# Hybrid decoder layer: the mixer's gates, queries and keys in seven-product groups

## The chip, the cores and the metric

The kernel runs on one core of a Trainium2 chip. The metric is the device time of one execution in microseconds (us). A core has five engines with queues of their own: TensorE (PE in the profile, its weight loads PEld), VectorE (DVE), ScalarE (ACT), GpSimd (POOL) and SyncE (SP). Each engine takes its instructions strictly in the order in which they were placed, and waits where an instruction's inputs or its output buffer are not ready. Transfers between DRAM and the on-chip memory are issued by SP and POOL.

## The reference, cut to what matters

One layer over 256 tokens of width 2048: a feed-forward half step (FFN), a mixer with two attention branches, a second FFN, each followed by a layer norm of the residual sum. Everything is float32. The mixer:

```python
def _mixer(h, positions, w_in, ...):
    c_q, c_kv, k_r, dq, dk, dv, gate_mla, gate_diff = _split_columns(h @ w_in)   # 512, 512, 64, 1024, 1024, 1024, 2048, 2048
    q = (_rms_norm(c_q, q_norm_g) @ w_uq).reshape(b, s, MLA_HEADS, MLA_QK_DIM)   # then rope on a part
    c_kv = _rms_norm(c_kv, kv_norm_g)
    k_nope = (c_kv @ w_uk).reshape(...)
    v_mla = (c_kv @ w_uv).reshape(...)
    ...
    o_mla = _mla_attention(q, k, v_mla).reshape(b, s, MLA_V_COLS)
    o_diff = _diff_attention(dq, dk, dv, positions, lam)                         # reshaped by heads
    o_diff = (_rms_norm(o_diff, subln_g) * (1.0 - lambda_init)).reshape(b, s, DIFF_V_COLS)
    y = jax.nn.sigmoid(gate_mla) * (o_mla @ w_br_mla) + jax.nn.sigmoid(gate_diff) * (o_diff @ w_br_diff)
    return y @ w_out
```

## The kernel before, in words

**Products.** A float32 product is made of three passes: activations and weights are each split into a rounded part `hi` and a rest `lo`, and `triple` (lines 201 to 204) multiplies hi by hi, hi by lo and lo by hi into one PSUM bank. The split of a weight tile of 128 x 1024 (`split`, lines 148 to 150) is a copy on ScalarE (L149) and a subtraction on VectorE (L150). Activations (128 tokens of one half b) are the stationary operand, weights the moving one, 512 columns wide.

**Units.** `project` (L206) goes over one chunk of 512 columns in units of two input tiles (G = 2): load of 512 KB by SyncE into one of four `raw` buffers, split into a pair of the ring (`wring`), then 12 matmuls: 2 tiles x 2 token halves x 3 passes. A chunk over the whole width of 2048 (16 tiles, KD) is 8 units, a chunk over 512 (4 tiles) is 2. `unit`, `advance` and `look` (lines 167 to 190) keep two queues: `look(3, 4)` makes the program place loads three units ahead of the split, and splits four units ahead of the matmuls; with `look(0, 0)` they stand directly one behind the other. Engines run ahead of each other in any case as far as the ring (six pairs in the mixer, after `narrow_to(6)`) allows.

**Due times.** `later(n, fn)` puts work off by n units, `tick` runs it. A planner then orders the instructions of each engine by its own estimate of when their inputs are ready, so that a piece that is due later may be placed earlier on an engine.

**Seven products.** `Hybrid` (L290) takes two chunks of 512 columns together. Over the first 8 of 16 input tiles it treats tokens, inputs and columns as 2 x 2 blocks and forms seven block products in place of eight (`Seven`, L249, prepares the sums of activation blocks from the float32 copies `x.raws`; weight blocks are added on VectorE, L333). The other 8 tiles go by plain units. The raw weight blocks 11, 12, 21 and 22 of 128 x 1024 have two buffers each (`sraw`), and partial banks are kept as snapshots (`snap`, L310 and L311, copies on ScalarE). `group` runs 14 half products and 8 plain units. Both FFNs use it for their gate and up weights; `Folded` is a like scheme for the down weights, in which block 21 shares block 12's buffers (additions at L434).

**Memory.** `act_tile` gives one of 40 slots of 128 x 1024 floats, `tmp_tile` one of 6 slots of 128 x 512. PSUM has 5 banks for products and 3 for the rest.

**Turning.** Rows (tokens on partitions) become columns through DRAM: `turn` (L533) transposes 32 x 32 blocks on VectorE (L525), stores them by four POOL transfers (L527, `turn<-blocks`), loads them back (L539, `turned<-turn`), and then copies or splits them (L547, or `put`).

**The mixer** (L839) runs in this order: the compressed rows c_q (chunk `wc0`) and c_kv with k_r (`wc1`, `wc2`), normalized and turned at once into `cn`; diff queries `dqT` (2 chunks); `wuq` (3 chunks of 2 units), `wuk`, `wuv`; then diff keys `dkT`, diff values `dv`; then `gate(0)`, `gate(1)`, and for f = 0 to 3 `branch(f)` followed by `gate(f + 2)`. Each gate is two chunks (`wgm`, `wgd`), kept in an `act_tile` until its branch multiplies it in. The pieces of the attention heads (`mla_head`, `diff_head`) are strewn between the units by `later`. All of it goes by plain `project`.

Of the kernel before, what the change touches and what calls it, by code (L numbers as in the profile page):

```python
# [18 lines left out]
P = 128  # L19
# [40 lines left out]
def layer_kernel(ctx: ExitStack, tc: tile.TileContext, a: dict, out: bass.AP):  # L60
# [102 lines left out]
    def catch_up(n):  # L163
        while len(behind) > n:
            behind.popleft()()
# [124 lines left out]
    class Hybrid:  # L290


        def __init__(self, x, seven, k_tiles):
            self.x, self.seven, self.k_tiles = x, seven, k_tiles
            self.raws = {n: [act_tile([P, 1024], F32, "sraw") for _ in range(2)] for n in ("11", "12", "21", "22")}
            self.snaps = [[act_tile([P, 2, 512], F32, "snap") for _ in range(2)] for _ in range(2)]
            self.turn = 0

        def group(self, w0, w1, done):
            banks = {}  # L300
            snap = [t[:, i, :] for t in self.snaps[self.turn % 2] for i in range(2)]
            self.turn += 1
            n1, n2, n3, q5 = snap
            R = self.raws
# [534 lines left out]
    def mixer(x):  # L839
# [2 lines left out]
        gain = act_tile([P, 1024], F32, "gain")  # L842
        nc.gpsimd.dma_start(gain, a["c_gain"].partition_broadcast(P))
        cn = Acts(8, "cn")
        krT = act_tile([P, 2, T], F32, "krT")

        def c_norm(b, i):
            c = c_row[b][:, i * RANK:(i + 1) * RANK]
            junk = tmp_tile([P, RANK], "junk")
            ss = sm(1, "ss")  # L850
            S.activation(junk, c, AF.Square, accum_out=ss)
            ms = sm(1, "ms")
            V.tensor_scalar(out=ms, in0=ss, scalar1=1.0 / RANK, scalar2=None, op0=ALU.mult)
            r = rstd(ms, RMS_EPS, 1)
            V.scalar_tensor_tensor(out=c, in0=c, scalar=r, in1=gain[:, i * RANK:(i + 1) * RANK],
                                   op0=ALU.mult, op1=ALU.mult)
            later(2, lambda: turn_to_quad(c, b, cn, i, 4, 8))

        def cq_done(b, bank):
            S.copy(c_row[b][:, 0:RANK], bank)  # L860
# [27 lines left out]
            project(w, xx, kt, 512, done, k0)  # L888
            return dst

        def rows_proj(ws, xx, kt, name, k0=0):
            dst = [act_tile([P, 1024], F32, name) for _ in range(2)]

            def done(c, b, bank):
                S.copy(dst[b][:, c * 512:(c + 1) * 512], bank)
            for c in range(2):
                project(ws[c], xx, kt, 512, lambda b, bank, c=c: done(c, b, bank), k0)
            return dst
# [12 lines left out]
        v = rows_proj(a["wuv"], cn, 4, "v", 4)  # L911

        om = Acts(MH, "om")
        od = Acts(MH, "od")
# [96 lines left out]
        def gate(f):  # L1011
            for i, w in enumerate((a["wgm"], a["wgd"])):
                gt = act_tile([P, 2, 512], F32, "gate")

                def done(b, bank, gt=gt):
                    S.copy(gt[:, b, :], bank)
                project(w[f], x, KD, 512, done)
                gates[f, i] = gt

        yq = Acts(KD, "y")  # L1020

        def branch(f):
            g0, g1 = gates[f, 0], gates[f, 1]

            def done0(b, bank):
                V.tensor_tensor(out=g0[:, b, :], in0=bank, in1=g0[:, b, :], op=ALU.mult)

            def done1(b, bank):
                V.tensor_tensor(out=g1[:, b, :], in0=bank, in1=g1[:, b, :], op=ALU.mult)
                V.tensor_tensor(out=g0[:, b, :], in0=g0[:, b, :], in1=g1[:, b, :], op=ALU.add)  # L1030
                if f < 2:
                    later(1, lambda: turn_to_quad(g0[:, b, :], b, yq, f, 4, 6))
                else:
                    later(2, lambda: rows_to_quad(g0[:, b, :], b, yq, f))
            catch_up(0)
            for t in (g0, g1):
                S.activation(t, t, AF.Sigmoid)
            project(a["wbm"][f], om, MH, 512, done0)
            project(a["wbd"][f], od, MH, 512, done1)
# [138 lines left out]
```

## Time and profile before

| what | value |
|---|---|
| median of three runs | 2008.99 us (2007.35 to 2014.54) |
| profiled execution | 2005.43 us, its span 2003.7 us |
| TensorE busy | 1987.9 us, 99% |
| VectorE busy | 1629.5 us, 81% |
| ScalarE busy | 1191.2 us, 59% |
| GpSimd busy | 238.7 us, 12% |
| DRAM traffic | 455.25 MB, mean 227 GB/s |

The first FFN takes about the first 690 us, the mixer lasts until about 1190, the output projection until about 1300, and the second FFN fills the rest. Rows by stretch give the busy time of each engine with its number of instructions in brackets, then the granted TensorE clock, the share of the transfer engines, and GB/s. Rows in order of time give start and duration in us; in square brackets stands how long the engine was idle before the row and what it waited for. Matmuls are pipelined, so their durations overlap; the steps from start to start tell what one costs.

### The profile page before, as it was taken

What the parts mean: (1) busy time and instruction counts of PE and PEld (TensorE: products, weight loads), DVE (VectorE), ACT (ScalarE), POOL (GpSimd) and SP (SyncE); (2) the same over time, 40 slices, a digit from 0 to 9 for tenths busy, and PEclk for the clock granted to TensorE, in tenths of its full rate; (3) what the DMA queues carried; (4) which work ended last, traced back from release to release, by engine and by line L of the source; (5) the groups of instructions that cost most, each with busy time, mean ns of one, the idle gap of its engine ahead of it and who ended that gap; (6) DMA issues with size and microseconds to landing.
All of it is one profiled execution on the core that took longest, in us unless ns stands there. A gap on an engine that the chain in (4) does not pass through costs nothing.

```text
span 2003.7 us, 25261 instructions
## 1 busy us (share of the span) xinstructions
PE 1987.9 (99%) x8928; PEld 1646.3 (82%) x8928; DVE 1629.5 (81%) x1922; ACT 1191.2 (59%) x1503; POOL 238.7 (12%) x443
## 2 busy tenths in 40 slices
PE   9999999999999999999999999999999999999997
PEld 7888888888888898788888888888888888888886
DVE  8999999998897676565665555699999999987875
ACT  6666666666655564555764444466666666665551
POOL 0111001012100013520001100001110110121000
PEclk9999999999999999999999999999999999999999
DMA  8667656668777667864456675666676666588673
GB/s 325 218 225 266 236 193 217 222 200 279 269 270 234 201 216 242 288 226 157 148 179 215 213 276 189 218 223 230 223 268 230 198 215 230 195 290 288 220 241 112
DMA packets 132048, 455.25 MB, mean 227 GB/s; under 512 B 19105, under 2 KB 19153, under 8 KB 131921
## 3 DMA queue, kind: packets, MB, share of 16 engines
q1 hardware_dynamic: 109296, 389.59, 57.0%
q0 software_dynamic: 22624, 64.04, 10.3%
q8 instruction: 70, 1.15, 0.2%
q14 instruction: 58, 0.47, 0.1%
HBM read 428.92 MB, written 24.64 MB: 226 GB/s over the span
## 4 chain that ended last, share of the span: by engine, by line
PE 91%; DMA 4%; DVE 1%; issue 1%; ACT 1%; POOL 1%; SPq 0%; DVEq 0%; ACTq 0%; POOLq 0%
PE mm L204 29%; PE mm L202 29%; PE mm L203 29%; DMA turn<-blocks 2%; DMA turned<-turn 1%; PE tr L202 1%; PE tr L203 1%; PE tr L204 1%; POOL turn L527 1%; DVE wring L150 1%; ACT wring L149 1%; DMA raw<-in_wdq_dram 1%; PE tr L490 0%; DMA raw<-in_wdk_dram 0%; DMA raw<-in_gu_dram 0%
## 5 line engine op out<-in xcount | busy, mean ns | idle before, releaser
L150 DVE TENSOR_TENSOR wring<-raw,wring 128x1024 fp32r<-128x1024 f32 (+2 forms) x551 | 660.8, 1205 | 263.3 <-ACT wring L149 257.1
L149 ACT CAST wring<-raw 128x1024 fp32r<-128x1024 f32 (+2 forms) x551 | 570.0, 1040 | 417.6 <-PE mm L204 322.3
L202 PE MATMUL mm<-wring,h 128*128 128x512 f32 (+2 forms) x1504 | 584.5, 389 | 0.0
L204 PE MATMUL mm<-wring,h 128*128 128x512 f32 (+2 forms) x1504 | 580.1, 386 | 0.0
L203 PE MATMUL mm<-wring,h 128*128 128x512 f32 (+2 forms) x1504 | 579.2, 385 | 0.0
L149 ACT CAST wring<-sraw 128x1024 fp32r<-128x1024 f32 x336 | 349.8, 1053 | 147.9 <-PE mm L204 93.3
L150 DVE TENSOR_TENSOR wring<-sraw,wring 128x1024 fp32r<-128x1024 f32 x336 | 403.4, 1218 | 9.6 <-ACT wring L149 5.0
L204 PEld LDWEIGHTS mm<-wring,h 128*128 128x128 f32 x1504 | 282.4, 188 | 57.5 <-DVE h L150 1.0
L202 PEld LDWEIGHTS mm<-wring,h 128*128 128x128 f32 x1504 | 282.6, 188 | 56.0 <-ACT h L149 1.0
L203 PEld LDWEIGHTS mm<-wring,h 128*128 128x128 f32 x1504 | 282.6, 188 | 55.6 <-DVE wring L150 0.2
L202 PE MATMUL mm<-wring,xs 128*128 128x512 f32 x608 | 236.5, 389 | 0.0
L203 PE MATMUL mm<-wring,xs 128*128 128x512 f32 x608 | 236.5, 389 | 0.0
L204 PE MATMUL mm<-wring,xs 128*128 128x512 f32 x608 | 236.5, 389 | 0.0
L333 DVE TENSOR_TENSOR sraw<-sraw,sraw 128x1024 f32<-128x1024 f32 x160 | 192.3, 1212 | 0.0
L527 POOL DMA_DIRECT2D hT<-blocks x176 | 95.9, 553 | 759.6 <-DVE blocks L525 705.3
L203 PE MATMUL mm<-wring,x 128*128 128x512 f32 x384 | 149.7, 390 | 0.6 <-DVE wring L150 0.6
L202 PE MATMUL mm<-wring,x 128*128 128x512 f32 x384 | 149.4, 390 | 0.6 <-ACT wring L149 0.6
L204 PE MATMUL mm<-wring,x 128*128 128x512 f32 x384 | 149.3, 389 | 0.0
L203 PEld LDWEIGHTS mm<-wring,xs 128*128 128x128 f32 x608 | 114.1, 188 | 23.7
L202 PEld LDWEIGHTS mm<-wring,xs 128*128 128x128 f32 x608 | 114.1, 188 | 23.7
L204 PEld LDWEIGHTS mm<-wring,xs 128*128 128x128 f32 x608 | 114.1, 188 | 23.7
L527 POOL DMA_DIRECT2D turn<-blocks x104 | 56.9, 554 | 305.6 <-DVE blocks L525 261.3
(252 smaller groups left out, 1850.3 us busy)
## 6 DMA issues: line engine op xcount, KB each, us to landing
raw<-in_gu_dram SPq DMA_DIRECT2D x191, 512.0 KB, 4.3
sraw<-in_gu_dram SPq DMA_DIRECT2D x160, 512.0 KB, 5.3
raw<-in_dn_dram SPq DMA_DIRECT2D x144, 512.0 KB, 4.5
hraw<-hT POOLq DMA_DIRECT2D x80, 256.0 KB, 4.7
sraw<-in_dn_dram SPq DMA_DIRECT2D x32, 512.0 KB, 5.5
raw<-in_wgm_dram SPq DMA_DIRECT2D x32, 512.0 KB, 3.3
raw<-in_wgd_dram SPq DMA_DIRECT2D x32, 512.0 KB, 3.8
raw<-in_w_out_dram SPq DMA_DIRECT2D x32, 512.0 KB, 3.4
```

Source lines behind the costliest of these rows:

```text
L149: S.copy(hi, src)
L150: V.tensor_tensor(out=lo, in0=src, in1=hi.bitcast(F32), op=ALU.subtract)
L202: PE.matmul(o, xh, wh, start=first, stop=False, skip_group_check=again)
L203: PE.matmul(o, xh, wl, start=False, stop=False, skip_group_check=again)
L204: PE.matmul(o, xl, wh, start=False, stop=last, skip_group_check=again)
L333: V.tensor_tensor(out=t, in0=t, in1=R[add[1]][s], op=ALU.add)
L527: nc.gpsimd.dma_start(to.rearrange("(g r) (i f) -> i r g f", g=4, i=4)[i], t[32 * i:32 * (i + 1), :].rearrange("r (g f) -> r g f", g=4))
```

## The change

The mixer opens differently. After the compressed rows, the first halves of the two gates (chunks 0 and 1 of `wgm` and of `wgd`), the diff queries and the diff keys go as four pairs of chunks through `Hybrid`. For this the activations of the first two quarters are kept in float32 (`h1 = Acts(KD, "h1", (0, 1))`), and the sums of `Seven` are made while the compressed rows are projected. `Hybrid` gets a `small` form: block 21 shares block 12's two buffers, there is one set of snapshots, and the last three products come in the order 3, 2, 4. `look(3, 4)` holds for the four groups, `look(0, 0)` after them.

All gates (16 tiles of 128 x 512) go to DRAM and are loaded again before their branch. The compressed rows also wait in DRAM, and are loaded and split during the first half of the diff values, which now stands ahead of `wuq`; the second half follows after `wuv`, then the other halves of the gates by plain `project`. A branch is divided: `branch_mla` copies its product to a tile, `branch_diff` multiplies in both gates and adds. The due times of the heads change.

```diff
-        def __init__(self, x, seven, k_tiles):
+        def __init__(self, x, seven, k_tiles, small=False):
+
             self.x, self.seven, self.k_tiles = x, seven, k_tiles
-            self.raws = {n: [act_tile([P, 1024], F32, "sraw") for _ in range(2)] for n in ("11", "12", "21", "22")}
-            self.snaps = [[act_tile([P, 2, 512], F32, "snap") for _ in range(2)] for _ in range(2)]
+            self.raws = {n: [act_tile([P, 1024], F32, "sraw") for _ in range(2)] for n in ("11", "12", "22")}
+            self.raws["21"] = self.raws["12"] if small else [act_tile([P, 1024], F32, "sraw") for _ in range(2)]
+            self.snaps = [[act_tile([P, 2, 512], F32, "snap") for _ in range(2)] for _ in range(1 if small else 2)]
+            self.last = (3, 2, 4) if small else (2, 4, 3)
...
-            for p, n, j in ((1, 0, 4), (5, 0, 5), (6, 0, 6), (7, 0, 7), (2, 1, 4), (4, 1, 5), (3, 1, 6)):
+            for p, n, j in zip((1, 5, 6, 7) + self.last, (0, 0, 0, 0, 1, 1, 1), (4, 5, 6, 7, 4, 5, 6)):
...
+        turns = {}
+        seven = Seven(x.raws)
+        for i, f in enumerate(seven.steps):
+            later(14 + 2 * i, f)
...
-            later(2, lambda: turn_to_quad(c, b, cn, i, 4, 8))
+            turns[i, b] = dram.tile([P, 512], F32, name=nm("turn"))
+            later(2, lambda: turn_out(c, turns[i, b]))
...
+        gate_rows = dram.tile([4, 2, 2, P, 512], F32, name="gates")
+
+        def keep_gate(i, f, b, bank, snap=None, op=None):
+            t = tmp_tile([P, 512], "gate")
+            if snap is None:
+                S.copy(t, bank)
+            else:
+                V.tensor_tensor(out=t, in0=bank, in1=snap, op=op)
+            nc.gpsimd.dma_start(gate_rows[f, i, b], t)
+
+        look(3, 4)
+        hy = Hybrid(x, seven, KD, True)
+        for i, w in enumerate((a["wgm"], a["wgd"])):
+            hy.group(w[0], w[1], lambda n, b, bank, snap, op, i=i: keep_gate(i, n, b, bank, snap, op))
+
+        def pair_cols(w, name):
+            dst = [act_tile([P, 4, T], F32, name) for _ in range(2)]
+
+            def done(n, b, bank, snap, op):
+                t = tmp_tile([P, 512], name + "r")
+                V.tensor_tensor(out=t, in0=bank, in1=snap, op=op)
+                later(1, lambda: turn_to_cols(t, dst[n], b, 4, 10))
+            hy.group(w[0], w[1], done)
+            return dst
+
+        dqT = pair_cols(a["wdq"], "dqT")
+        dkT = pair_cols(a["wdk"], "dkT")
+        look(0, 0)
...
-        dqT = [cols_proj(a["wdq"][c], x, KD, "dqT") for c in range(2)]
+        def c_back(j):
+            if j == 0:
+                for key, src in turns.items():
+                    back[key] = tmp_tile([P, 512], "turned")
+                    nc.gpsimd.dma_start(back[key], src)
+            if j >= 4:
+                i, b = divmod(j - 4, 2)
+                cn.put(i, b, turned(back[i, b]))
+
+        dv, dv_part = rows_proj("dv")
+        dv_part(a["wdv"], x, KD, 0, 0, c_back)
...
-                later(12 + 3 * h + 2 * i, f)
-        dkT = [cols_proj(a["wdk"][c], x, KD, "dkT") for c in range(2)]
-        dv = rows_proj(a["wdv"], x, KD, "dv")
+                later(10 + 3 * h + 2 * i, f)
...
-                later(4 + 6 * h + 3 * i, f)
+                later(22 + 6 * h + 3 * i, f)
...
+        for f, at in enumerate((44, 48, 56, 60)):
+            later(at, lambda f=f: get_gates(f))
+
+        dv_part(a["wdv"], x, KD, 1)
+        for i, w in enumerate((a["wgm"], a["wgd"])):
+            for f in (2, 3):
+                project(w[f], x, KD, 512, lambda b, bank, i=i, f=f: keep_gate(i, f, b, bank))
...
-        gate(0)
-        gate(1)
-        for f in range(4):
-            branch(f)
-            if f + 2 < 4:
-                gate(f + 2)
+        for f in range(3):
+            branch_mla(f)
+        branch_diff(0)
+        branch_diff(1)
+        branch_mla(3)
+        branch_diff(2)
+        branch_diff(3)
...
-    h1 = Acts(KD, "h1")
+    h1 = Acts(KD, "h1", (0, 1))
```

More of the change, by code (lines that the diff above doesn't have):

```diff
@@ L300, in group @@
             banks = {}
-            snap = [t[:, i, :] for t in self.snaps[self.turn % 2] for i in range(2)]
+            snap = [t[:, i, :] for t in self.snaps[self.turn % len(self.snaps)] for i in range(2)]
             self.turn += 1
@@ new lines, in rows_proj, with part, done @@
+        def rows_proj(name):
+            dst = [act_tile([P, 1024], F32, name) for _ in range(2)]
+            def part(ws, xx, kt, c, k0=0, hook=None):
+                def done(b, bank):
+                    S.copy(dst[b][:, c * 512:(c + 1) * 512], bank)
+                project(ws[c], xx, kt, 512, done, k0, hook)
+            return dst, part
+        back = {}
+        def c_back(j):
[6 more added lines that the diff above has]
+                cn.put(i, b, turned(back[i, b]))
@@ L910, in mixer @@
         kT = [cols_proj(a["wuk"][c], cn, 4, "kT", 4, 8) for c in range(2)]
-        v = rows_proj(a["wuv"], cn, 4, "v", 4)
+        v, v_part = rows_proj("v")
+        for c in range(2):
+            v_part(a["wuv"], cn, 4, c, 4)
         om = Acts(MH, "om")
@@ L1020, in mixer, with get_gates @@
-        yq = Acts(KD, "y")
[L1022 to L1035, printed above, removed]
+        def get_gates(f):
+            gates[f] = [act_tile([P, 2, 512], F32, "gate") for _ in range(2)]
+            for i, t in enumerate(gates[f]):
+                for b in range(2):
+                    nc.gpsimd.dma_start(t[:, b, :], gate_rows[f, i, b])
@@ L1036, in branch, with branch_diff, done @@
+        def branch_diff(f):
+            g0, g1 = gates.pop(f)
+            y = mla_rows.pop(f)
             for t in (g0, g1):
                 S.activation(t, t, AF.Sigmoid)
-            project(a["wbm"][f], om, MH, 512, done0)
-            project(a["wbd"][f], od, MH, 512, done1)
-        gate(0)
-        gate(1)
-        for f in range(4):
-            branch(f)
-            if f + 2 < 4:
-                gate(f + 2)
+            def done(b, bank):
+                V.tensor_tensor(out=y[:, b, :], in0=y[:, b, :], in1=g0[:, b, :], op=ALU.mult)
+                V.tensor_tensor(out=g1[:, b, :], in0=bank, in1=g1[:, b, :], op=ALU.mult)
+                V.tensor_tensor(out=y[:, b, :], in0=y[:, b, :], in1=g1[:, b, :], op=ALU.add)
+                if f < 2:
+                    later(1, lambda: turn_to_quad(y[:, b, :], b, yq, f, 4, 6))
+                else:
+                    later(2, lambda: rows_to_quad(y[:, b, :], b, yq, f))
+            project(a["wbd"][f], od, MH, 512, done)
```

17 lines of the change are left out of this document (4 added, 13 removed).

## The prediction

> **What bounds the kernel now.** I read the profile's page first (busy shares, slices), then the busy time by stretch, then single engines in order of time, and last the waits.
>
> ```profile
> span 2003.7 us, 25261 instructions
> PE 1987.9 (99%) x8928; PEld 1646.3 (82%) x8928; DVE 1629.5 (81%) x1922; ACT 1191.2 (59%) x1503; POOL 238.7 (12%) x443
> PEclk9999999999999999999999999999999999999999
> ```
> ```profile
> core 0: us, PE busy (x) PEld busy (x) DVE busy (x) ACT busy (x) POOL busy (x), PEclk, DMA share, GB/s
> 400.00:450.00 50.00, 50.00 (x222) 41.38 (x222) 48.79 (x54) 32.95 (x39) 6.55 (x12) 1.00 0.61 204
> 710.00:750.00 40.00, 40.00 (x257) 37.47 (x256) 26.76 (x56) 24.15 (x46) 6.60 (x12) 1.00 0.73 240
> 780.00:790.00 10.00, 9.14 (x40) 7.04 (x39) 1.88 (x2) 3.72 (x5) 1.14 (x2) 1.00 0.53 205
> 1100.00:1150.00 50.00, 50.00 (x222) 41.42 (x221) 28.41 (x29) 23.05 (x26) 6.04 (x11) 1.00 0.65 205
> ```
> ```profile
> 700.00:1200.00 500.00, 497.40 (x2336) 414.92 (x2335) 303.48 (x479) 274.65 (x425) 80.13 (x146) 1.00 0.66 216
> ```
>
> TensorE bounds every stage. The stretch at 400 lies in the first FFN's hybrid groups, where VectorE is 98% busy; the one at 1100 lies in the mixer's gates, where VectorE is 57% busy; both pass 222 matmuls in 50 us. So a VectorE at 98% does not yet slow TensorE here. In the mixer (700 to 1200) TensorE is idle for only 2.6 us in all.
>
> What one matmul is worth is not its duration:
>
> ```profile
> 1099.77 0.39 PE L203 MATMUL mm<-wring,h 128*128 128x512 f32 x1
> ...
> 1101.36 0.39 PE L204 MATMUL mm<-wring,h 128*128 128x512 f32 x1
> ```
>
> Seven starts follow each other in 1.59 us between these rows: 0.227 us per matmul, while each lasts 0.39. Pricing by the duration would overstate the gain 1.7 times.
>
> **The change, part by part.**
>
> *Matmuls.* Two chunks of 512 columns over 16 input tiles cost 2 x 16 x 2 halves x 3 products = 192 matmuls. A hybrid group costs 7 x 4 x 3 = 84 for the first eight tiles and 96 for the rest: 180. Four groups save 48; in the instruction order of the two programs 8424 matmuls of 512 columns become 8376 and every other TensorE count stays. 48 x 0.227 = **10.9 us** off the bounding engine.
>
> *VectorE and ScalarE.* A group splits 22 weight tiles where 16 were split, and adds 8 pairs of weight tiles.
>
> ```profile
> L150 DVE TENSOR_TENSOR wring<-sraw,wring 128x1024 fp32r<-128x1024 f32 x336 | 403.4, 1218 | 9.6 <-ACT wring L149 5.0
> L333 DVE TENSOR_TENSOR sraw<-sraw,sraw 128x1024 f32<-128x1024 f32 x160 | 192.3, 1212 | 0.0
> L647 DVE TENSOR_TENSOR gus<-mm,snap 128x512 f32<-128x512 f32 x80 | 54.6, 682 | 0.0
> L525 DVE STREAM_TRANSPOSE blocks<-dqTr 128x512 f32<-128x512 f32 x4 | 2.8, 702 | 0.0
> L149 ACT CAST wring<-sraw 128x1024 fp32r<-128x1024 f32 x336 | 349.8, 1053 | 147.9 <-PE mm L204 93.3
> L310 ACT COPY snap<-mm 128x512 f32<-128x512 f32 x40 | 23.3, 583 | 9.9 <-PE mm L204 9.9
> ```
> ```profile
> 426.09 3.49 DVE L150 TENSOR_TENSOR wring<-sraw,wring 128x1024 fp32r<-128x1024 f32 x3
> ```
>
> Neighbours overlap: three splits take 3.49 us, so each after the first adds (3.49 - 1.22) / 2 = 1.135, 0.08 less than its duration; I take 0.08 off the others too. A gate group then needs 30 x 1.135 + 4 x 0.60 = 36.5 us of VectorE against 180 x 0.227 = 40.9 of TensorE (89%). A group of queries or keys adds 4 transposes of 0.62: 38.9 us (95%). An FFN group by the same sum has 36.5 + 4 x 0.34 + 2 x 0.61 = 39.1 (96%), and there the row above shows no loss. ScalarE needs 22 x 0.97 + 4 x 0.5 = 23 us, little over half. The five preparation steps of the products (four subtractions, three splits, a negation: about 6.4 us of VectorE by the same prices) fall into 710 to 750, where VectorE has 13.2 us free in the row above. Inside the first group also fall the norm and rotation of the second compressed half, about 6.5 us. So over four groups VectorE has 163.6 - 36.5 x 2 - 38.9 x 2 - 6.5 = 6.3 us to spare, besides its lead: four units prepared ahead, at 40.9 / 22 units = 7.4 us. If that cover were gone, every further microsecond is TensorE's.
>
> *Fewer raw buffers.* Block 21 now uses block 12's buffers, product 4 moves to the end so that block 11's buffers come free last, and there is one set of snapshots. A refill cannot be issued before the last split of the old content, and SyncE's queue holds the later loads behind it.
>
> ```profile
> raw<-in_gu_dram SPq DMA_DIRECT2D x191, 512.0 KB, 4.3
> sraw<-in_gu_dram SPq DMA_DIRECT2D x160, 512.0 KB, 5.3
> raw<-in_wgm_dram SPq DMA_DIRECT2D x32, 512.0 KB, 3.3
> raw<-in_wuq_dram SPq DMA_DIRECT2D x6, 512.0 KB, 5.7
> turn<-blocks POOLq DMA_DIRECT2D x104, 64.0 KB, 4.2
> turned<-turn POOLq DMA_DIRECT2D x26, 256.0 KB, 4.7
> ```
> ```profile
> L328 SPq DMA_DIRECT2D sraw<-in_gu_dram x160: 327/328/553, 32.8 to 1704.7; - x160
> ```
> ```profile
> DVE sraw L434 <- DMA sraw<-in_dn_dram: 14.1, 9, 4.4
> ```
>
> In the built program 4 to 6 VectorE instructions (4.5 to 6.8 us) stand between release and use of the shared pair, 3 to 4.5 (3.4 to 5.1 us) for block 11 across a group's end. Landing takes 5.3 us and the issue itself 0.33. That leaves about 0.4 us late for each of four shared refills and 1.4 for each of three refills of block 11: 6 us of VectorE waiting in all. Bounds: 0 (landing 3.3) to 7 x 3 = 21 us. The down stage shares the same buffers; its VectorE waits up to 4.4 us a time (last row), and TensorE loses nothing there.
>
> The Trainium skill, "DMA: Bandwidth & Descriptors", section "Latency and other measured facts", has memory latency rise from 0.2 us on average to 2 us at high load. By that rule each of the seven refills would be up to 1.8 us later, 12.6 us of waiting in place of 6, and the sum below some 6 us worse. The trace goes the same way: equal loads land in 3.3 us for the gates and 5.7 for the query weights.
>
> *Turned rows.* Compressed rows go to DRAM and come back under half of the diff values (8 units of 2.7 us) instead of just before their use. That removes a stall:
>
> ```profile
> 786.28 0.62 ACT L547 COPY dqT<-turned 128x512 f32<-128x512 f32 x1 [8.98 <-DMA turned<-turn]
> ```
> ```profile
> 787.88 1.23 DVE L150 TENSOR_TENSOR wring<-raw,wring 128x1024 fp32r<-128x1024 f32 x1 [9.32 <-ACT wring L149]
> ```
> ```profile
> 787.41 0.39 PE L204 MATMUL mm<-wring,h 128*128 128x512 f32 x1
> 787.90 0.50 PE L202 MATMUL mm<-wring,cn 128*128 128x512 f32 x1
> 789.16 0.50 PE L203 MATMUL mm<-wring,cn 128*128 128x512 f32 x1 [0.76 <-DVE wring L150]
> ```
>
> ScalarE waits 9.0 us for turned diff queries, all splits queue behind it, VectorE waits 9.3, and TensorE starts two matmuls late by 0.49 - 0.23 and 1.26 - 0.23: 1.3 us. The lead was about four units of 2.7 us, 10.9 us. The wait does not vanish: the same copies of diff queries now stand in ScalarE's queue in the middle of the key group, where units average 1.86 us and the lead is 7.4. A transposed block needs a store (4.2) and a load (4.7) behind POOL's own queue; by the built order I expect about 8 us of ScalarE waiting there.
>
> *Gates through DRAM.* 16 stores and 16 loads of 256 KB (8.4 MB, under 2% of the traffic) and 8 copies of branch rows on ScalarE (0.58 each). The loads are issued 8 units, 21.8 us, ahead of a 4.7 us landing: nothing. Exposed wholly, four pairs of loads would cost 4 x 4.7 = 19 us. POOL issues 32 x 0.55 = 18 us more (0.55: 6.60 us for 12 in the stretch at 710); it is 16% busy in the mixer. Moving branches, heads and the halves of diff values reorders equal TensorE work: nothing, bounded by the 2.6 us idle now on one side and by some 1 us per late head on the other.
>
> *Sum.* Waiting in the hybrid stage, 6 + 8 = 14 us, meets 6.3 spare + 7.4 lead = 13.7, but the waits bunch in the last group: I take **+2 us** of TensorE stall, between 0 (all covered) and +14 (none); nearest is the 1.3 us that a 9 us wait cost above. With -1.3 for the stall removed: -10.9 - 1.3 + 2 = **-10.2 us**. The profiled execution took 2005.43 us (span 2003.7), giving 1995.2; the median of the runs, 2008.99, stands 3.6 higher, giving **1998.8**.
>
> **The rivals.**
>
> *A, all waits covered.* Every stall in the mixer goes: -10.9 - 2.6 = -13.5, 1995.5. For it: an FFN group at 98% loses nothing. Against: fewer buffers than there.
>
> *B, the waits outrun the lead.* Refills land late in each group and TensorE loses 5 to 14 us: 2002 to 2011, middle 2005. For it: the 5.7 us landings under load. Against: the down stage's 14.1 us of such waits cost nothing. The Trainium skill, "Perfetto Trace Analysis", section "Identifying Performance Opportunities", reads a gap that keeps repeating on the saturated engine as too little on-chip memory for the next tile; by that rule giving up buffers speaks for B. No such gap is in this trace.
>
> *C, slower.* The refill loop (last split, issue, landing, next add) paces the stage. Ten refills of pairs (four of 21, three of 12, three of 11), each late by e: stall 10e + 8 - 13.7. Over 0.5% slower needs a stall of 22 us, so e above 2.8, a landing of about 8 us instead of 5.3. At e = 3.5 the stall is 29 us and the time 2008.99 - 12.2 + 29.3 = 2026. Against: VectorE never waited over 4.4 us for such a load.
>
> *D, no smaller TensorE work* is excluded by the count of 48.
>
> **How the numbers follow.** A measurement of this kernel tells about 0.5%, 10 us, from no change: under 1998.9 counts as faster, over 2019 as slower. Forecast 0.60 (1995 to 2002), A 0.10, B 0.22, C 0.08. The forecast lies on the line, a little over half of it below: faster 0.10 + 0.36 = 0.46, slower 0.08, same 0.46. The range leaves out C and the upper end of B, and reaches 2.5 us below A for the spread of the runs: 1993 to 2008.
>
> **What would show it.** Right: TensorE 512-wide matmuls down by 48; start to start still 0.227 in the hybrid groups; VectorE near 90% busy in the gate groups and 95% after; ScalarE's wait for turned diff queries inside the key group; no TensorE gap at the first use of the compressed rows. Wrong: TensorE waits on splits repeating once a group (B, C), VectorE waits on raw loads above 2 us each, the shared refill landing above 8 us, or a TensorE gap at the start of the first group, where the preparation steps and the first nine loads meet.

## The result and the profile after

The changed kernel takes 1994.26 us (median of six runs, 1992.62 to 1994.81) against 2008.57 us (2003.96 to 2014.54) for the kernel before: a ratio of 0.9927, with a 95% interval of 0.9911 to 0.9943. The time went the way that was forecast and lies in the range, 4.5 us under the forecast; it is 0.7 us below the 1995 to 2002 that the working gave the forecast itself. The profiled execution took 1994.06 us, its span 1992.2. Two things show at once: the profiled spans differ by 11.5 us and the medians by 14.3, and the runs now lie within 2.2 us of each other where they lay 10.6 us apart.

The page of the changed kernel, its span, its busy engines and the weight additions:

```profile
span 1992.2 us, 25364 instructions
PE 1977.3 (99%) x8880; PEld 1638.4 (82%) x8880; DVE 1704.0 (86%) x2002; ACT 1220.5 (61%) x1537; POOL 256.0 (13%) x475
L336 DVE TENSOR_TENSOR sraw<-sraw,sraw 128x1024 f32<-128x1024 f32 x192 | 231.6, 1217 | 0.5 <-DMA sraw<-in_wgm_dram 0.3
```

TensorE has 8880 instructions where it had 8928, the 48 fewer of the working, and its busy time fell by 10.6 us. VectorE took 32 more additions of weight blocks and 24 more splits, and is 74.5 us busier, with no change in TensorE's share.

The busy time in the four groups, cut where TensorE passes from one group to the next (columns as in the same view of before):

```profile
744.00:787.00 43.00, 42.89 (x194) 35.09 (x193) 40.51 (x61) 27.35 (x37) 5.47 (x10) 1.00 0.78 269
787.00:829.00 42.00, 40.81 (x181) 33.38 (x180) 38.83 (x37) 25.19 (x27) 2.17 (x4) 1.00 0.65 224
829.00:870.00 41.00, 41.00 (x182) 33.97 (x181) 38.83 (x37) 24.76 (x26) 5.12 (x10) 1.00 0.70 236
870.00:911.00 41.00, 41.00 (x182) 33.98 (x181) 38.58 (x39) 27.70 (x31) 9.74 (x18) 1.00 0.66 206
```

VectorE, which works some four units ahead, is 94, 92, 95 and 94% busy. TensorE is idle for 1.2 us in the second group and for 0.1 in the first. The waits of VectorE in these four groups (744 to 911), and then of TensorE in the whole mixer (700 to 1220), in us in total, times, longest:

```profile
DVE wring L150 <- ACT wring L149: 9.3, 8, 2.5
```
```profile
PE mm L203 <- DVE wring L150: 1.2, 1, 1.2
PE tr L493 <- DVE mla L1089: 1.2, 1, 1.2
```

VectorE waits 9.3 us in the groups. TensorE has two stalls of more than half a microsecond left in the mixer. The first stands in the second group and begins at its border to the first; in order of time, SyncE's issues, ScalarE (this border and the two after it, then its wait for turned diff queries), VectorE and TensorE:

```profile
774.59 4.33 SPq L331 DMA_DIRECT2D sraw<-in_wgd_dram  x3
```
```profile
781.11 1.05 ACT L149 CAST wring<-sraw 128x1024 fp32r<-128x1024 f32 x1 [4.04 <-DMA sraw<-in_wgd_dram]
...
820.97 1.05 ACT L149 CAST wring<-sraw 128x1024 fp32r<-128x1024 f32 x1 [2.48 <-DMA sraw<-in_wdq_dram]
...
860.34 1.05 ACT L149 CAST wring<-sraw 128x1024 fp32r<-128x1024 f32 x1 [1.05 <-DMA sraw<-in_wdk_dram]
...
876.67 0.62 ACT L550 COPY dqT<-turned 128x512 f32<-128x512 f32 x1 [2.41 <-DMA turned<-turn]
```
```profile
782.19 1.22 DVE L150 TENSOR_TENSOR wring<-sraw,wring 128x1024 fp32r<-128x1024 f32 x1 [2.49 <-ACT wring L149]
```
```profile
793.91 0.39 PE L202 MATMUL mm<-wring,xs 128*128 128x512 f32 x1
795.49 0.50 PE L203 MATMUL mm<-wring,xs 128*128 128x512 f32 x1 [1.19 <-DVE wring L150]
```

Block 11 of the second group is loaded when the last split of the first group's block 11 has read the buffer. Its first half is the issue at 774.59 (the first of the three in the row), which lands 6.5 us later: ScalarE has waited 4.0 us for it, VectorE 2.5. VectorE then works without a pause, and some twelve microseconds on TensorE comes 1.58 - 0.23 = 1.35 us late for a split. At the next two borders ScalarE waits 2.5 and 1.1 us for the same block, and TensorE loses nothing. The second stall is at the end of the last branch; the first compressed rows, where 1.3 us went before, follow without a step:

```profile
1201.01 0.39 PE L204 MATMUL mm<-wring,od 128*128 128x512 f32 x1
1202.57 0.63 PE L493 MATMUL tr<-ident,mla 128*128 128x128 f32 x4 [1.17 <-DVE mla L1089]
```
```profile
931.21 0.39 PE L204 MATMUL mm<-wring,h 128*128 128x512 f32 x1
931.43 0.39 PE L202 MATMUL mm<-wring,cn 128*128 128x512 f32 x1
```

### The profile page after: what moved, and what is told of

Same layout as the page of the kernel before. It is cut to its first block, busy times and chain, and to the rows that moved or that the text cites. A ratio compares the mean times of both kernels' runs of the same rounds, so it can differ in the third digit from the quotient of the medians.

```text
span 1992.2 us, 25364 instructions
## 1 busy us (share of the span) xinstructions
PE 1977.3 (99%) x8880; PEld 1638.4 (82%) x8880; DVE 1704.0 (86%) x2002; ACT 1220.5 (61%) x1537; POOL 256.0 (13%) x475
## 4 chain that ended last, share of the span: by engine, by line
PE 95%; DVE 2%; DMA 2%; issue 1%; ACT 0%; SPq 0%; DVEq 0%; POOL 0%; ACTq 0%
PE mm L204 30%; PE mm L203 30%; PE mm L202 30%; DVE wring L150 1%; PE tr L204 1%; PE tr L202 1%; PE tr L203 1%; DMA raw<-in_w_out_dram 0%; PE tr L493 0%; DMA sraw<-in_wgm_dram 0%; DMA sraw<-in_wgd_dram 0%; DMA raw<-in_gu_dram 0%; PE tr L976 0%; PE tr L1005 0%; PE tr L974 0%
## 5 line engine op out<-in xcount | busy, mean ns | idle before, releaser
L150 DVE TENSOR_TENSOR wring<-raw,wring 128x1024 fp32r<-128x1024 f32 (+2 forms) x519 | 622.9, 1206 | 188.3 <-ACT wring L149 181.9
L149 ACT CAST wring<-raw 128x1024 fp32r<-128x1024 f32 (+2 forms) x519 | 538.2, 1041 | 367.8 <-PE mm L204 272.2
L202 PE MATMUL mm<-wring,h 128*128 128x512 f32 (+2 forms) x1376 | 532.4, 387 | 0.0
L204 PE MATMUL mm<-wring,h 128*128 128x512 f32 (+2 forms) x1376 | 530.2, 386 | 0.0
L203 PE MATMUL mm<-wring,h 128*128 128x512 f32 (+2 forms) x1376 | 529.7, 385 | 0.0
L149 ACT CAST wring<-sraw 128x1024 fp32r<-128x1024 f32 x392 | 408.4, 1054 | 180.2 <-PE mm L204 98.6
L150 DVE TENSOR_TENSOR wring<-sraw,wring 128x1024 fp32r<-128x1024 f32 x392 | 471.2, 1221 | 15.0 <-ACT wring L149 10.2
L204 PEld LDWEIGHTS mm<-wring,h 128*128 128x128 f32 x1376 | 258.5, 188 | 52.4 <-DVE h L150 1.4
L202 PEld LDWEIGHTS mm<-wring,h 128*128 128x128 f32 x1376 | 258.5, 188 | 51.3 <-ACT h L149 1.0
L203 PEld LDWEIGHTS mm<-wring,h 128*128 128x128 f32 x1376 | 258.6, 188 | 51.1 <-DVE wring L150 0.2
L203 PE MATMUL mm<-wring,xs 128*128 128x512 f32 x720 | 280.4, 389 | 1.3 <-DVE wring L150 1.2
L202 PE MATMUL mm<-wring,xs 128*128 128x512 f32 x720 | 280.3, 390 | 0.0
L204 PE MATMUL mm<-wring,xs 128*128 128x512 f32 x720 | 280.1, 389 | 0.0
L336 DVE TENSOR_TENSOR sraw<-sraw,sraw 128x1024 f32<-128x1024 f32 x192 | 231.6, 1217 | 0.5 <-DMA sraw<-in_wgm_dram 0.3
L203 PEld LDWEIGHTS mm<-wring,xs 128*128 128x128 f32 x720 | 135.2, 188 | 30.0 <-DVE wring L150 2.1
L202 PEld LDWEIGHTS mm<-wring,xs 128*128 128x128 f32 x720 | 135.1, 188 | 28.5 <-ACT wring L149 0.3
L204 PEld LDWEIGHTS mm<-wring,xs 128*128 128x128 f32 x720 | 135.2, 188 | 28.0
L203 PEld LDWEIGHTS mm<-wring,x 128*128 128x128 f32 x384 | 72.1, 188 | 16.1 <-DVE wring L150 1.2
```

Of the source, the lines that this page charges most:

```text
L149: S.copy(hi, src)
L150: V.tensor_tensor(out=lo, in0=src, in1=hi.bitcast(F32), op=ALU.subtract)
L202: PE.matmul(o, xh, wh, start=first, stop=False, skip_group_check=again)
L203: PE.matmul(o, xh, wl, start=False, stop=False, skip_group_check=again)
L204: PE.matmul(o, xl, wh, start=False, stop=last, skip_group_check=again)
L336: V.tensor_tensor(out=t, in0=t, in1=R[add[1]][s], op=ALU.add)
```

## The experiments

Each set of runs had runs of the kernel before beside it on the same chip: 2007.83 us (median of 21, 2004.76 to 2014.00) beside E1 to E4, 2006.03 (12, 2002.30 to 2012.01) beside E5 to E8, 2007.39 (15, 2005.73 to 2013.33) beside E9 to E12. Their medians differ by up to 2.5 us from set to set; what is said below of a variant against the changed kernel's 1994.26 us, which was taken in a set of its own, is uncertain by about as much.

**E1. The order without the block products.**

```diff
-        seven = Seven(x.raws)
-        for i, f in enumerate(seven.steps):
-            later(14 + 2 * i, f)
...
-        hy = Hybrid(x, seven, KD, True)
+        class Plain:
+            def group(self, w0, w1, done):
+                for n, w in enumerate((w0, w1)):
+                    project(w, x, KD, 512, lambda b, bank, n=n: done(n, b, bank, None, None))
+        hy = Plain()
...
-                V.tensor_tensor(out=t, in0=bank, in1=snap, op=op)
+                S.copy(t, bank)
```

> The changed order is kept, but the four pairs of chunks go by plain units (192 matmuls each in place of 180) and the sums of activation blocks are left out; the outputs stay whole. If the smaller TensorE work carries the gain: 48 matmuls x 0.227 = 10.9 us come back, less the 1.6 us that TensorE now loses in the groups (1.35 at 793.9, 0.28 at 757.1): span about 1992.2 + 9.3 = 2001.5 us, 0.3% to 0.6% slower than the changed kernel. If the new order carries it (the stall at the first compressed rows and the spread of the runs go with the order): span below 1997 us, and the median within 3 us of the changed kernel's 1994.3.

Measured: 2003.08 us (2001.98 to 2005.79, ten runs), ratio 0.9978 (0.9969 to 0.9987). The span of the profile is 2000.6 us; the stretch of the four pairs:

```profile
744.00:920.00 176.00, 176.00 (x783) 145.94 (x782) 89.11 (x101) 81.28 (x96) 26.37 (x49) 1.00 0.73 232
```

VectorE is 51% busy there and TensorE loses nothing. The block products are worth 2003.08 - 1994.26 = 8.8 us, and 8.4 in the spans: 10.9 less the changed kernel's stalls. But the rest of the change without them, called the order from here on, is worth 2007.83 - 2003.08 = 4.75 us, and the spread of the runs (3.8 us) went with it. Both theories held a part.

**E2. Only the copies of the diff queries later, in the kernel before.**

```diff
-        dqT = [cols_proj(a["wdq"][c], x, KD, "dqT") for c in range(2)]
+        dqT = [cols_proj(a["wdq"][c], x, KD, "dqT", 0, 13) for c in range(2)]
```

> The kernel before, with one number changed: the diff queries' turned rows are copied 13 units after their load in place of 10. If the 9 us wait of ScalarE for them makes the stall at the first compressed rows, and its length from run to run makes the 10 us spread of the runs before: that wait and the 1.3 us stall go, span about 2002.4 us, the runs within 3 us of each other and their median 3 to 5 us below before. If the spread has another cause: span 2002.4 us at best and the same spread, median within 1.5 us of before.

Measured: 2003.73 us (2002.08 to 2005.53, twelve runs), ratio 0.9975 (0.9966 to 0.9985): 4.1 us and the spread are gone with one number. But the mechanism was not the one expected. ScalarE still waits as long for the first of these rows, and here TensorE loses nothing by it:

```profile
784.76 0.62 ACT L547 COPY dqT<-turned 128x512 f32<-128x512 f32 x1 [8.85 <-DMA turned<-turn]
```

Up to this place both programs have the same instructions in the same order. What the number changes comes after: the copies of the first queries now stand ahead of the second half of the diff queries, and between them, in ScalarE's queue. TensorE has no wait at the first attention head, where E5 will show one.

**E5. The kernel before, unchanged, profiled a second time.**

> The kernel before, unchanged: a second profiled execution. The profile shown was a fast one (2005.43 us against a median near 2008), and the run with later copies of the diff queries kept the same program up to 795 us, where the stall at the first compressed rows was 1.3 us in one execution and 0 in the other. If waits for turned rows make the spread of the runs: whatever this execution takes above 2003 us is TensorE idle between 780 and 880 us, behind ScalarE waiting for turned rows. If the spread comes from elsewhere: the idle time in that stretch stays at 2.5 to 3.5 us and the rest lies in another stage.

Measured: 2004.23 us, span 2002.5. At the first compressed rows TensorE's starts are 0.23 us apart, and 0.31 once, where they were 0.49 and 1.26:

```profile
787.54 0.39 PE L202 MATMUL mm<-wring,cn 128*128 128x512 f32 x1
787.77 0.48 PE L203 MATMUL mm<-wring,cn 128*128 128x512 f32 x1
788.08 0.39 PE L204 MATMUL mm<-wring,cn 128*128 128x512 f32 x1
```

But another stall has grown: TensorE waits for the first attention head's softmax, which needs the turned keys. First the row of the first profiled execution of the kernel before, then of this one:

```profile
867.84 0.39 PE L204 MATMUL mm<-wring,h 128*128 128x512 f32 x1
868.91 0.70 PE L834 MATMUL tr<-ident,p 128*128 128x128 f32 x3 [0.69 <-DVE p L929]
```
```profile
865.60 0.39 PE L204 MATMUL mm<-wring,h 128*128 128x512 f32 x1
867.81 0.70 PE L834 MATMUL tr<-ident,p 128*128 128x128 f32 x3 [1.82 <-DVE p L929]
```

The same program has a gap of 1.3 and one of 0.85 us in one execution, 0.1 and 2.0 in the other. Both executions lie below the medians of their sets; none of the longest (2008 to 2014 us) was profiled.

**E9. Only the first heads later, in the kernel before.**

```diff
-                later(12 + 3 * h + 2 * i, f)
+                later(15 + 3 * h + 2 * i, f)
```

> The kernel before, with the attention heads of the first kind due three units (8.2 us) later; all turned rows stay in their places. Two executions of the kernel before had TensorE waiting 0.85 and 1.98 us for the first head's softmax, whose keys come last out of the row of turned blocks. If that wait, which differs from run to run, makes the kernel's spread and 4 us of its median: median 3 to 5 us below before, runs within 4 us of each other, no TensorE gap over 0.5 us at the first softmax transposes. If the stall at the first compressed rows makes them: median less than 1.5 us below before and a spread above 6 us.

Measured: 2004.43 us (2003.06 to 2006.46, eleven runs), ratio 0.9984 (0.9975 to 0.9993). 3.0 us and more than half of the spread go (3.4 us against 7.6), and the first transposes of the softmax follow with no wait:

```profile
876.68 0.39 PE L204 MATMUL mm<-wring,h 128*128 128x512 f32 x1
876.96 0.70 PE L834 MATMUL tr<-ident,p 128*128 128x128 f32 x3
```

All turned rows kept their places here, so what moved with these heads carries some 3 us of the median of the kernel before, and half of its spread. The first head's wait is the one that the two profiles show, with 0.85 and 2.0 us; that it makes the whole 3 us is argued from there.

**E12. The same heads earlier, in the changed kernel.**

```diff
-                later(10 + 3 * h + 2 * i, f)
+                later(8 + 3 * h + 2 * i, f)
```

> The changed kernel with the heads of the first kind due two units (5.4 us) earlier. If the changed kernel's small spread comes from slack between the turned keys and the first head: a gap of 0.5 to 4 us at the first softmax transposes and runs that differ by more than 3 us. If the slack is above 5.4 us: no gap there, median within 1 us of 1994.3 and runs within 2.5 us.

Measured: 1994.16 us (1992.35 to 1997.78, five runs), ratio 0.9935 (0.9923 to 0.9948); TensorE has no wait at the first heads in its profile. The slack is above 5.4 us there; one run of five at 1997.78 leaves open whether it always is.

**E4. Product 4 summed into block 21's buffer.**

```diff
-                    7: (None, "12", ("12", "22"), "X"), 2: ("21", "21", None, "Y"), 4: (None, "11", ("11", "21"), "W"),
+                    7: (None, "12", ("12", "22"), "X"), 2: ("21", "21", None, "Y"), 4: (None, "21", ("21", "11"), "W"),
```

> Product 4 adds blocks 11 and 21 in place into block 21's buffer in place of block 11's, so that block 11 comes free with the addition, one split (1.1 us) and what lies between earlier: about 2.3 us. If the late refill of block 11 makes the stall of 1.35 us at 793.9: ScalarE's waits of 4.0 and 1.05 us for the second group's first block fall by about 2 us each, the stall goes, span about 1990.8 us. If the shared buffer of 12 and 21, which now comes free later, is as tight: the wait moves to the addition of product 5 and the span stays within 0.5 us of 1992.2.

Measured: 1992.63 us (1990.73 to 1994.10), ratio 0.9921 (0.9909 to 0.9934). ScalarE's wait for the second group's first block, and TensorE's only wait for a split between 757 and 800:

```profile
781.73 1.06 ACT L149 CAST wring<-sraw 128x1024 fp32r<-128x1024 f32 x1 [1.73 <-DMA sraw<-in_wgd_dram]
```
```profile
PE mm L203 <- DVE wring L150: 0.3, 1, 0.3
```

4.0 became 1.7 us and the stall behind the border is gone: it was block 11's late refill. The other profiles agree. Without this edit ScalarE waited there for 3.4 (E12), 3.9 (E11) and 4.1 us (E7), and TensorE came 0.7, 1.2 and 1.6 us late; with it (E8 and E10) ScalarE waited for 1.4 us, and TensorE had no stall. The profiled span, 1992.1, doesn't show the gain, because a gap of 1.5 us at 549 us took its place in that execution; it lies in the down weights of the first FFN, which the edit doesn't touch. (The edit does reach the gate and up groups of both FFNs; TensorE has no wait in them in either profile.) The medians differ by 1.6 us, but the intervals of the two ratios overlap, so the gain in time isn't shown.

**E3. The last products in the order 2, 4, 3.**

```diff
-            self.last = (3, 2, 4) if small else (2, 4, 3)
+            self.last = (2, 4, 3)
```

> The last three products in the order 2, 4, 3 in place of 3, 2, 4. The shared buffer is then refilled between products 7 and 2, some 3 VectorE instructions (3.4 us) against an issue of 0.33 and a landing of 5.2 us: about 2.1 us late in each of four groups, while block 11 gets more time. If the late refills pace the groups: VectorE waits 8 to 10 us more for block loads over the four groups and TensorE loses 2 to 6 us more, span 1994 to 1998 us. If the lead of four units covers a wait of 2 us a group: the stall at the border of the first two groups (1.35 us) goes and nothing takes its place, span about 1991 us.

Measured: 1993.78 us (1992.37 to 1994.60), span 1991.3. It says nothing on its question. Loads are placed three units ahead of the split, so in this order block 21 is loaded into the shared buffer before product 7 has read block 12 there: product 7 multiplies other weights, and no refill waits for it. What it does show is what the order 3, 2, 4 is for: it keeps more than three units between the last use of 12 and the load of 21. The tight refill (case C) wasn't tried in another way.

**E6. Half of the lead.**

```diff
-        look(3, 4)
+        narrow_to(4)
+        look(3, 2)
         hy = Hybrid(x, seven, KD, True)
...
         look(0, 0)
+        set_ring(6)
```

> The changed kernel with four pairs in the ring and two units prepared ahead in the four groups, in place of six and four: the lead falls from 7.4 to 3.7 us. If waits of VectorE add up over a group and are met by spare time and lead together, as the prediction had it: TensorE loses 3 to 6 us more in the groups, span 1995 to 1998 us. If only a single wait longer than the lead counts (the longest was 2.5 us): under 1 us more, span below 1993.2 us.

Measured: 2000.35 us (1996.97 to 2002.33, seven runs), ratio 0.9964 (0.9952 to 0.9976): 6.1 us slower than the changed kernel. TensorE goes through the four groups from 744.5 to 918.8 us, where the changed kernel took from 744.3 to 911.0. VectorE's wait for its first split, and its waits for splits in the groups after that (744 to 919):

```profile
742.28 1.23 DVE L150 TENSOR_TENSOR wring<-sraw,wring 128x1024 fp32r<-128x1024 f32 x1 [3.79 <-ACT wring L149]
```
```profile
DVE wring L150 <- ACT wring L149: 12.2, 14, 1.5
```

With 1.9 us for two additions that is 14.1 us in the groups, against 9.3 in the changed kernel. The stretches of the four groups, summed, in this kernel and then in the changed one:

```profile
sum 175.00, PE 170.23 PEld 137.45 DVE 158.38 ACT 105.97 POOL 23.99; mean PE 42.56 PEld 34.36 DVE 39.59 ACT 26.49 POOL 6.00
```
```profile
sum 167.00, PE 165.69 PEld 136.42 DVE 156.75 ACT 105.00 POOL 22.50; mean PE 41.42 PEld 34.10 DVE 39.19 ACT 26.25 POOL 5.62
```

TensorE is idle for 4.8 us there in place of 1.3, and some 1.8 us more go at a lower clock (last section). Of the 4.8 us, 2.8 lie in the first group, and so does the lower clock; there the first wait, 3.8 us, was by itself as long as the 3.7 us of lead that are left. In the other three groups no wait of VectorE exceeds 1.5 us, and still TensorE is idle for 2.0 us, in five places. There waits below the lead do add up. Whether the sum or the single wait made the greater loss in the first group, this run doesn't separate.

**E7. The copies of queries and keys earlier.**

```diff
-                later(1, lambda: turn_to_cols(t, dst[n], b, 4, 10))
+                later(1, lambda: turn_to_cols(t, dst[n], b, 4, 4))
```

> The changed kernel with the turned diff queries and keys copied 4 units after their load in place of 10: in the key group 7.4 us in place of 18.6. If the copies' place in ScalarE's queue is what kept its wait at 2.4 us where the prediction had 8: ScalarE waits 6 to 10 us for turned rows in the key group, the splits queue behind it, and TensorE loses 1 to 4 us, span 1993 to 1996 us. If transfers land early enough anyway: the wait stays below 4 us and the span within 0.5 us of 1992.2.

Measured: 1995.01 us (1993.11 to 1995.84, four runs), ratio 0.9936 (0.9920 to 0.9952), span 1993.6. ScalarE's wait for the diff queries stays where it was (2.3 us after 2.4); a new one, for the keys, stands behind the groups, among the plain units of the diff values:

```profile
918.63 0.62 ACT L550 COPY dkT<-turned 128x512 f32<-128x512 f32 x1 [4.67 <-DMA turned<-turn]
```

TensorE has no gap there (its gaps, 1.6 and 0.8 us, are at 795 and 758). So 4.7 us in ScalarE's queue are covered where four units of lead are worth 4 x 2.7 = 10.9 us. Within the groups, where they are worth 7.4, the edit didn't lengthen the wait, and its question stays open there.

**E11. The gates loaded one unit before use.**

```diff
-        for f, at in enumerate((44, 48, 56, 60)):
+        for f, at in enumerate((51, 55, 63, 67)):
```

> The changed kernel with each branch's gate rows loaded one unit ahead of the branch in place of eight. If the eight units (21.8 us) are what hides the loads: ScalarE waits 4 to 8 us for gates at each of four branches, the splits queue behind, and TensorE loses 5 to 20 us, span 1997 to 2012 us. If the ring's lead covers the wait: span below 1994 us.

Measured: 1997.52 us (1997.14 to 1998.64, four runs), ratio 0.9952 (0.9939 to 0.9966). In the profile only the last of the four branches shows it, in ScalarE's wait and TensorE's:

```profile
ACT gate L1084 <- DMA gate<-gates: 4.5, 1, 4.5
```
```profile
PE tr L493 <- DVE mla L1089: 3.6, 1, 3.6
```

So the loads that lie in the open cost 3.3 us, part of it at a lower clock (last section), and not the 19 of the working: at the other three branches ScalarE has no wait for a gate. The eight units are worth that much; nothing of them is exposed in the changed kernel.

**E8. The diff values as a fifth group**, with E4's edit, the head pieces and gate loads moved up by about eight units.

```diff
-        dv, dv_part = rows_proj("dv")
-        dv_part(a["wdv"], x, KD, 0, 0, c_back)
+        dv = [act_tile([P, 1024], F32, "dv") for _ in range(2)]
+        for j in range(8):
+            later(6 + 2 * j, lambda j=j: c_back(j))
+        hy.group(a["wdv"][0], a["wdv"][1], lambda n, b, bank, snap, op: V.tensor_tensor(
+            out=dv[b][:, n * 512:(n + 1) * 512], in0=bank, in1=snap, op=op))
+        look(0, 0)
...
-                later(10 + 3 * h + 2 * i, f)
+                later(10 + 5 * h // 2 + 2 * i, f)
...
-                later(22 + 6 * h + 3 * i, f)
+                later(14 + 6 * h + 3 * i, f)
...
-        for f, at in enumerate((44, 48, 56, 60)):
+        for f, at in enumerate((36, 40, 48, 52)):
...
-        dv_part(a["wdv"], x, KD, 1)
```

> The changed kernel with the diff values as a fifth group of block products, product 4 summed into block 21's buffer, and the heads eight units earlier. If TensorE's count carries on to pay: 12 matmuls fewer (2.7 us) and the stall at the border of the groups gone (about 1.5 us in the medians): median about 1990.0 us, span about 1988 us. If the heads, with eight units less to hide behind, take it back: median 1992 to 1996 us, with idle TensorE between 950 and 1100 us before softmax transposes.

Measured: 1990.86 us (1989.56 to 1992.93, five runs), ratio 0.9918 (0.9903 to 0.9932).

```profile
PE 1974.4 (99%) x8868; PEld 1635.5 (82%) x8868; DVE 1721.3 (86%) x2020; ACT 1224.1 (61%) x1543; POOL 255.2 (13%) x475
```

Twelve matmuls went, and the median is the lowest of all, 3.4 us under the changed kernel's; the two weren't run beside each other, and the intervals of their ratios to the kernel before overlap.

**E10. The same, with the second norm's rows loaded later.**

```diff
-    ln = LayerNorm(1.0, res[0], a["ln2_g"], a["ln2_b"], keep(1), h2, a["ln2_cols"])
+    ln = LayerNorm(1.0, res[0], a["ln2_g"], a["ln2_b"], keep(1), h2, a["ln2_cols"], ((2, 3, 9, 11), (13, 15, 17, 19)))
```

> The kernel with the diff values as a fifth group and product 4 summed into block 21's buffer, with the loads of the second layer norm's rows spread later over the output projection (units 2, 3, 9, 11 in place of 0, 2, 4, 6). If these 2 MB beside the first output weights made the weights land late and the gap of 1.7 us at the last branch: the gap falls below 0.5 us and the median by 1 us, to 0.991 of before. If the gap comes from the chain of gate products alone: it stays above 1.2 us and the ratio at 0.992.

Measured: 1991.98 us (1990.59 to 1993.65, five runs), ratio 0.9921 (0.9908 to 0.9935). The gap at the last branch stays (a wait of 1.7 us in its profile, 1.5 in E8's): the loads beside the output weights don't make it. Nor does the chain of gate product and addition by itself: in E12's profile the same chain leaves a gap of 0.3 us. VectorE in the changed kernel, then VectorE and TensorE in E12 (L1088 is the gate product, 1200.33 the branch's last matmul):

```profile
1199.87 1.23 DVE L150 TENSOR_TENSOR wring<-raw,wring 128x1024 fp32r<-128x1024 f32 x1 [0.73 <-ACT wring L149]
1201.02 0.68 DVE L1088 TENSOR_TENSOR gate<-mm,gate 128x512 f32<-128x512 f32 x1
```
```profile
1199.35 0.68 DVE L1088 TENSOR_TENSOR gate<-mm,gate 128x512 f32<-128x512 f32 x1
```
```profile
1200.33 0.39 PE L204 MATMUL mm<-wring,od 128*128 128x512 f32 x1
1200.90 0.63 PE L493 MATMUL tr<-ident,mla 128*128 128x128 f32 x4 [0.19 <-DVE mla L1089]
```

From the start of the gate product to the transposes it is 1.55 us in both, and 1.55 and 1.56 in E8 and E10. What differs is when VectorE comes to it, which is as soon as it has split a tile of the output weights: in E12 1.0 us before the branch's last matmul starts, in the changed kernel together with it, in E8 and E10 0.3 and 0.6 us after it. So the split ahead of the gate product makes the gap; why it stands later in some executions is open.

## Why the prediction was right

The time lies in the range, but not by the account that gave the forecast. It is 1.3 us above the lower end, which was put 2.5 us below rival A for the spread of the runs. A's 1995.5 us is the nearest of the figures, and A's account, every wait covered, isn't what the profile shows. The gain from the order was larger than the sum had it, and that the range still held was in part luck.

*Matmuls: right.* The count fell by 48, start to start stayed 0.227 (931.21 to 931.43 above), and E1 gives back 8.8 us by undoing it, the 10.9 less about 2 of stall.

*The stalls in the groups, +2 us: right in size and in the buffer named, wrong in the group.* 14 us of waits were forecast; VectorE waited 9.3. Block 11's refill at a group's end was put at 1.4 us late with a landing of 5.3; at the first border it landed in 6.5, which makes 2.6, and cost VectorE 2.5 and TensorE 1.35. But the working had the waits bunch in the last group, and TensorE lost nothing in the last two. The shared refills (0.4 late each) cost little: over the whole kernel VectorE's additions waited 0.3 us for a load of the first group. Two of the signs of being wrong came in a small way: one wait of VectorE above 2 us behind a load, and a gap of 0.28 us on TensorE early in the first group (757.6). ScalarE's wait for turned diff queries was put at 8 us and was 2.4, inside the key group as forecast. The comparison of the summed waits with spare time and lead (9.3 against 13.7) would have given no stall at all; one came all the same, so a sum over four groups is too coarse. E6 agrees with it in direction: with half the lead, 14.1 us of waits and 6.1 us more. The Trainium skill, "Perfetto Trace Analysis", section "Identifying Performance Opportunities", taken for case B, would have a gap return at every group; it came after one border of three, and E4 took it away without a buffer more.

*Gates through DRAM at nothing: right*, with 19 us as an upper end that E11 puts at 3.3.

*The branches, at nothing: short.* The divided branch ends in a stall that no term had, 1.3 us in this profile and 0.3 in E12's.

*The stall removed, -1.3 us: the step that failed, by its size.* "That removes a stall", the working said, and took it from one execution. The order was worth 4.75 us (E1). Most of this is not the stall at the first compressed rows: it is 1.3 us in one execution, 0.1 in E5 and nothing in E2 and E9, though ScalarE waits 8.8 to 9.0 us for the same rows in all four. E2 and E9 point to the first head's wait for turned keys (0.85 and 2.0), of which the working had only the 0.85, inside its 2.6 us of idle TensorE: each takes that wait out of the way of the kernel before, and they win 4.1 and 3.0 us.

*The step from the profile to the median failed with it.* The profiled execution of before lay 3.6 us under its median, and those 3.6 us were added to the forecast as if they would stay. They fit a wait that varies from run to run and that the change removed: the changed kernel's profiled execution lies 0.2 us under its median. By the working's own terms with -4.75 for the order in place of -1.3, the medians should differ by 10.9 + 4.75 - 2 = 13.7 us; they differ by 14.3.

What stays open is how much of the 4.75 us is this one wait, and where the longest executions of the kernel before lose 4 to 10 us, since none was profiled.

## What to carry to other kernels

When a kernel's runs spread by several microseconds and its profiled execution is one of the shortest, price a wait by the spread, not by the length that it happened to have: a chain that just arrives in time costs more in the median than in the profile, and an edit that gives it slack wins that too. E2 and E9 fit this, though no long execution was profiled. An engine at 94% may be given more work if its waits find spare time and lead to meet them; but look at the stretch in which the lead is used up, since a sum over the whole stage hid the one stall that came. And where a buffer is summed in place, choose the one whose next load is the less urgent: E4 took the stall away by that alone. Last, look at what stands ahead of a late instruction in its own queue, and not only at its chain: the gate product came late because of the split before it.

## What the runs showed of the hardware

A gap on TensorE can cost more than its length. In E11, after 3.7 us without a matmul, the rows by stretch show the granted clock (the number after POOL's) at half for about 3 us:

```profile
1194.00:1196.00 2.00, 1.25 (x5) 1.25 (x6) 2.00 (x3) 0.13 (x1) 0.00 (x0) 0.66 1.03 420
1196.00:1198.00 2.00, 2.00 (x6) 1.55 (x5) 1.97 (x3) 0.46 (x1) 0.00 (x0) 0.50 1.01 408
1198.00:1202.00 4.00, 4.00 (x20) 3.31 (x20) 2.02 (x4) 1.53 (x2) 0.00 (x0) 0.99 1.03 410
```

In E6 the same happened after three waits of 1.17, 0.44 and 0.28 us within 4 us, and matmuls then started 0.43 us apart in place of 0.227:

```profile
759.46 0.50 PE L202 MATMUL mm<-wring,xs 128*128 128x512 f32 x1 [1.17 <-ACT wring L149]
760.41 0.73 PE L202 MATMUL mm<-wring,h 128*128 128x512 f32 x2 [0.44 <-ACT wring L149]
761.43 0.64 PE L203 MATMUL mm<-wring,xs 128*128 128x512 f32 x1 [0.28 <-DVE wring L150]
...
763.15 0.63 PE L204 MATMUL mm<-wring,xs 128*128 128x512 f32 x1
763.57 0.63 PE L202 MATMUL mm<-wring,xs 128*128 128x512 f32 x1
```

The single gaps of 1.35 us in the changed kernel and of 2.0 us in E5 left the granted clock at 1.00. The Trainium skill, "TensorE: Matmul & The Clock Gate", section "What's actually happening", has half the clock after an idle window of about 3.4 us. E11 agrees; in E6 TensorE was idle for 1.9 us in all before it. Whether the longest executions of the kernel before lose their time in this way was not tried.
